# A hybrid recurrent decoder step on one core: norm rows made in columns, and the last weight group split into prompt and sample columns

## The chip, the cores and the metric

The kernel runs on one NeuronCore of a Trainium2 chip. Its engines are named as in the profile: PE is TensorE (matmul), PEld its weight load, DVE is VectorE, ACT is ScalarE, POOL is GpSimd, SP is SyncE, which mostly issues DMAs. The metric is the device time of one execution in microseconds (us); lower is better.

## The reference

One inference step of a two-layer decoder trunk over two groups of tokens: 256 prompt tokens with zero initial state, and 8 sequences of 8 sample tokens with given states. So there are 320 token columns, and the model width is 2048. All is float32.

- Layer 0: `h = rmsnorm(x)`, one input projection of `h` to 7,200 columns; eight gated-delta heads and four GLA heads run over it; `x += W_out[...]`.
- Layer 1: `h = rmsnorm(x)`, a projection to 4,096 columns (branch and gate), a convolution over 4 tokens, an RG-LRU scan, a gate; `x += W_out[...]`.
- `y = rmsnorm(x) * final_norm` for both groups, beside the new states.

The part that the change touches is the norm, three times:

```
def _rmsnorm(x, g):
    xf = x.astype(jnp.float32)
    y = xf * lax.rsqrt(jnp.mean(xf * xf, axis=-1, keepdims=True) + EPS)
    return (y * g.astype(jnp.float32)).astype(x.dtype)
```

## The kernel before

**Tiling.** Activations are kept transposed: the 2048 features lie on 128 partitions times 16 tiles, the 320 tokens along the free dimension (columns 0 to 255 prompt, 256 to 319 sample). The residual is `ob[m][:, f, :]`, four tiles of four blocks. All dense weights come as 30 groups of 512 output features; a group has 8 chunks of 2 feature tiles, 512 KB each. `run_group` (line 250) walks a group: for each chunk, for each of four 128-feature blocks `f`, for both tiles `a`, it issues one *product* (line 259).

**A product is three matmuls (line 265).** Weights and activations are split into a high and a low part in the fp32r type: `wh`, `wl` and `xh`, `xl`. The product is `wh*xh + wh*xl + wl*xh`, with the 128x128 weights stationary and 320 activation columns moving. The four blocks of a group accumulate in four PSUM banks (`acc`, four buffers). Weights are split on the fly by `split_chunk` (line 235): ScalarE writes `wh` (L240), VectorE writes `wl` (L241), two chunks ahead, into six buffers of each; SP loads chunks four ahead into three buffers (L210).

**Order of the work.** Everything beside the dense products is written as generators in four lists, `hi`, `lo`, `lo2` and `tails`. After each product there is a *slot* (line 130), which advances the first generator of each list by one step. `wait(name)` yields as many slots as the table `WAITS` says; with it the distance between the steps of a piece of side work is set. The instructions so written are then put in order for each engine by a planner, by priority and by its own costs; splits and evacuations have raised priority (`HP`, `HE`). Each engine executes its list in order, so that an instruction that waits holds back all behind it. `behind(i)` keeps a side matmul from being planned ahead of the latest product.

**The norms.** The gain is folded into the activations and the row of `1/rms` is applied to the products afterwards. The first two norms go through `row_rstd` (line 335): one matmul of all-ones weights over the summed squares gives each token's sum on all partitions, in 320 columns; ScalarE scales it and takes the root (L340, L341); VectorE takes the reciprocal (L343), and GpSimd refines it by a Newton step (L344 to L347). The first makes `rb0`, beside groups 0 and 1, and its first readers are L355 and L356 in `evac_padded` (line 352), which the convolution taps (L464) and ScalarE's L101 follow. The second makes `rb1`, needed at the end of the first group of layer 1. The row `rb0` is read also by all later evacuations of layer 0.

**The final norm and the tail.** `evac_fin` (line 1639) adds the residual (L1642) for the last four groups; for the last it squares each block (L1645). `last` (line 1680) sums the squares per token with the squares as weights (`sums`, L1677), so that tokens lie on partitions in three columns, raises them to -1/2 (L1686) and spreads them back over columns by `spread_rows` (line 326, L331). Lines 1919 to 1928 then multiply the sixteen blocks by that row, VectorE most of them (L1927), GpSimd two (L1923), each followed by its store (eight on SP's queue, one on ScalarE's).

Beside the last four groups run the GLA sample states (`sample_states(16, 24)`, line 992), with matmuls of their own at L1132; those of the delta states (L1118) ran beside earlier groups in the same way.

Of the kernel before, what the change touches and what calls it, by code (L numbers as in the profile page):

```python
# [7 lines left out]
F32 = mybir.dt.float32  # L8
# [63 lines left out]
def hybrid_step(ctx, tc, x_cols, w_dense, w_small, w_lr, w_gate, par_a, par_b, par_c, gains, head_rows,  # L72
# [21 lines left out]
    def bank(name):  # L94
        return psum.tile([P, 512], F32, name=name, tag="bg", bufs=4)

    def bank4(name):
        return psum.tile([P, 4, P], F32, name=name, tag="bg", bufs=4)

    def scaled(out, in_, scale):  # L100
        return act.activation(out, in_, AF.Identity, scale=scale)  # L101
# [64 lines left out]
    eps = const.tile([P, 1], F32, name="eps")  # L166
# [68 lines left out]
    def split_chunk(i, a):  # L235
        if i >= len(chunks):
            return
        h = wpool.tile([P, 512], F32R, name="wh", tag="wh", bufs=6)
        l = wpool.tile([P, 512], F32R, name="wl", tag="wl", bufs=6)
        act.activation(h, wst[i][:, a, :], AF.Copy)  # L240
        env["last_split"] = dve.tensor_sub(l, wst[i][:, a, :], h.bitcast(F32))  # L241
# [84 lines left out]
    def spread_rows(ps, r):  # L326


        for c in range(3):
            n, a = (P, 0) if c < 2 else (64, 64)  # L330
            mm = pe.matmul(ps[:, c * P:c * P + n], r[:, c:c + 1].to_broadcast([P, P]), ident[:, a:a + n],  # L331
                           start=True, stop=True)
            behind(mm)

    def row_rstd(v, t, sq, out, nm):

        ps = bank(nm + "ps")
        behind(pe.matmul(ps[:, :NT], ones, sq, start=True, stop=True))
# [4 lines left out]
        dve.reciprocal(out, out)  # L343
        pool.tensor_mul(t, out, out)  # L344
        pool.tensor_mul(t, t, v)
        pool.tensor_scalar(t, t, -0.5, 1.5, op0=OP.mult, op1=OP.add)
        pool.tensor_mul(out, out, t)  # L347
# [67 lines left out]
    def slab():  # L415
        return env["keep"].tile([P, 4, XA], F32, name="slab", tag="slab", bufs=1)
# [1028 lines left out]
    def evac_res(m):  # L1445
        st = {}

        def before():
            def load():
                st["x0"] = env["ws2"].tile([P, 4, NT], F32, name="x0r", tag="x0r", bufs=1)  # L1450
                yield from wait("resid.1")
                for f in (0, 2):
                    behind(sp.dma_start(st["x0"][:, f:f + 2], x_cols[m, :, f:f + 2]))
                    yield from wait("fill.2")
            tails.append(load())

        def evac(f, acc):
            if f == 0:
                drain(tails)
            dve.tensor_add(ob[m][:, f, :], acc[:, :NT], st["x0"][:, f, :])  # L1460

        def sumsq():
            ws = env["ws2"]
            sq = ws.tile([P, 4, NT], F32, name="sq", tag="sq", bufs=1)
            act.activation(sq, ob[m], AF.Square)
            yield from wait("evac_res_sumsq.1")
            if m == 0:
                env["sqa"] = ws.tile([P, NT], F32, name="sqa", tag="sqa", bufs=1)
                dve.tensor_reduce(env["sqa"], sq.rearrange("p f t -> p t f"), axis=mybir.AxisListType.X, op=OP.add)
            else:  # L1470
                s1 = ws.tile([P, NT], F32, name="sq1", tag="sq1", bufs=1)
                dve.tensor_reduce(s1, sq.rearrange("p f t -> p t f"), axis=mybir.AxisListType.X, op=OP.add)
                dve.tensor_add(env["sqa"], env["sqa"], s1)
            yield from wait("evac_res_sumsq.2")
            env["done"].add(("x", m))
            if m == 3:
                yield from row_rstd(sq[:, 0], sq[:, 1], env["sqa"], rb1, "r1")
# [160 lines left out]

    def evac_fin(m):
        def evac(f, acc):  # L1640
            x = ob[m][:, f, :]
            dve.tensor_add(x, acc[:, :NT], x)  # L1642
            if m == 3:
                sq = fin["sq"]
                i = act.activation(sq[:, f, :], x, AF.Square)  # L1645
                if f < 2:
                    dve.tensor_add(fin["sqa"], fin["sqa"], sq[:, f, :])
                else:
                    with tc.issue_after(i.ins):
                        gain(f - 2)  # L1650
                    if f == 3:
                        fin["last"] = i

        def gain(f):
            i = scaled(ob[3][:, f, :], ob[3][:, f, :], pb[:, 12 + f, 42:43])
            return i

        def work():
            sq = fin["sq"]
# [14 lines left out]
        def sums(sq, i):  # L1674
            for c in range(3):
                a = min(c * P, NT - P)
                pe.matmul(fin["ps"][:, c, :], sq[:, a:a + P], ones,  # L1677
                          start=(i == 0 and c == 0), stop=(i == 2), skip_group_check=True)

        def last():  # L1680
            fin["ps"] = bank4("fsp")
            for i, sq in enumerate((fin["sqa"], fin["sq"][:, 2, :], fin["sq"][:, 3, :])):
                sums(sq, i)
            fr = fin["fr"]
            dve.tensor_scalar(fr, fin["ps"][:, 0:3, 0], 1.0 / D, EPS, op0=OP.mult, op1=OP.add)
            pool.tensor_tensor(fr, fr, mhalf[:, :3], OP.pow)  # L1686
            fin["row"] = [bank("frow") for _ in range(2)]
            for ps in fin["row"]:
                spread_rows(ps, fr)
            with tc.issue_after(fin["last"].ins):  # L1690
                for f in (2, 3):
                    gain(f)
            yield

        def after():
            if m < 3:
                tails.append(work())
            else:
                drain(tails)
                hi.append(last())  # L1700
        return None, evac, after

    for m in range(4):
# [67 lines left out]
    def start_work():  # L1771
# [14 lines left out]
        yield from row_rstd(sums[:, 1], sums[:, 2], sums[:, 0], rb0, "r0")  # L1786
# [116 lines left out]
    shut(lru_p, mid_p)  # L1903
    fin_p, fw = opened("fin", "right")
    env["ws2"] = fw
    fin["fr"] = fw.tile([P, 3], F32, name="fr")
    fin["sqa"] = fw.tile([P, NT], F32, name="fsqa")
    fin["sq"] = slab().rearrange("p f w -> p (f w)")[:, :4 * NT].rearrange("p (f t) -> p f t", f=4)
    env["upd"] = fw
    lo.append(sample_states(16, 24))  # L1910
# [1 line left out]
    for k in range(2):  # L1912
        one(k)
    run_group(next(gi), rest)
    for _ in range(3):
        run_group(next(gi))
    drain(hi)
    drain(tails)
    drain(lo)
    row = fin["row"][0][:, :NT]  # L1920
    rows = fw.tile([P, NT], F32, name="frows")
    act.activation(rows, fin["row"][1][:, :NT], AF.Copy)
    pool.tensor_mul(ob[3][:, 0:2], ob[3][:, 0:2], rows[:, None, :].to_broadcast([P, 2, NT]))  # L1923
    act.dma_start(y_cols[3, :, 0:2], ob[3][:, 0:2])
    for m, f, n in ((0, 0, 1), (0, 1, 1), (0, 2, 2), (1, 0, 2), (1, 2, 2), (2, 0, 2), (2, 2, 2), (3, 2, 2)):
        t = ob[m][:, f:f + n]
        dve.tensor_mul(t, t, row[:, None, :].to_broadcast([P, n, NT]))  # L1927
        sp.dma_start(y_cols[m, :, f:f + n], t)
# [62 lines left out]
```

## Time and profile before

| | |
|---|---|
| median of 3 runs | 988.08 us (986.78 to 988.36) |
| the profiled execution's own time | 988.05 us |
| its span | 985.9 us |
| mean granted TensorE clock | 0.994 |
| DMA over the span | 171.62 MB, mean 174 GB/s |

How to read it: a row of a timeline has the start in us from the start of the span, the time taken, the engine, the line of the kernel, the operation, what it writes and reads, the shapes, how many instructions are merged in the row, and in brackets how long the engine stood idle before and what released it. A row of a group has, behind the bar, the busy time in us, the mean of one instruction in ns, and the idle time before. A row of a wait has the engine, tile and line that waited, who ended the wait, the total in us, the number of times and the longest. A plain float32 matmul shows as two instructions (two passes). Matmuls are pipelined, and the time shown for one is longer than the distance from one start to the next.

### The profile page before, as it was taken

The numbers are of one execution on the slowest core, as the hardware profiler recorded it, in microseconds if no ns is written. First come the engines' busy times: TensorE is split into PE (matmuls) and PEld (weight loads), VectorE is DVE, ScalarE is ACT, GpSimd is POOL, SyncE is SP. The second block draws the span as 40 slices with busy tenths as digits, with TensorE's granted clock in tenths as the row PEclk, the third lists the DMA queues.
The fourth block names the chain that finished last, engine by engine and source line by source line (L and its number), as shares of the span: only waits on it lengthen the run. The fifth ranks groups of instructions, "written<-read, shape, count | busy, mean of one in ns | idle before, by whom it ended". The sixth has DMA issues, their size and how long they took to land.

```text
span 985.9 us, 18789 instructions
## 1 busy us (share of the span) xinstructions
PE 968.4 (98%) x6917; PEld 951.9 (97%) x6917; DVE 708.9 (72%) x1485; ACT 534.7 (54%) x1084; POOL 216.6 (22%) x365
## 2 busy tenths in 40 slices
PE   9999999999999999999999999999999999999995
PEld 9988999999999999999979999999999999999995
DVE  7897887675555557689658789777969668876753
ACT  8556874456433454676523335447685885343441
POOL 6420027602182021120104234200010000042200
PEclk9999999999999999999999999999999999999998
DMA  8544345443546367444477886654545445588742
GB/s 307 171 133 136 111 140 170 140 126 122 142 150 166 98 212 234 125 120 140 164 249 254 254 264 222 228 161 140 159 123 191 129 128 161 170 245 267 255 151 106
DMA packets 65331, 171.62 MB, mean 174 GB/s; under 512 B 16884, under 2 KB 22536, under 8 KB 64728
## 3 DMA queue, kind: packets, MB, share of 16 engines
q1 hardware_dynamic: 60256, 160.35, 52.3%
q0 software_dynamic: 2720, 8.66, 2.5%
q10 hardware_dynamic: 2264, 1.42, 0.5%
q8 instruction: 54, 0.88, 0.4%
q14 instruction: 37, 0.30, 0.1%
HBM read 155.73 MB, written 14.68 MB: 173 GB/s over the span
## 4 chain that ended last, share of the span: by engine, by line
PE 86%; DVE 4%; ACT 3%; issue 3%; DMA 2%; POOL 1%; SPq 0%; DVEq 0%; ACTq 0%; POOLq 0%
PE acc L265 75%; DVE wl L241 1%; ACT wh L240 1%; DMA wst<-in_w_dense_dram 1%; DMA XT<-xt_scratch 1%; DVE ob L1927 0%; POOL xsums L1782 0%; PE gpo L1368 0%; PE lg L1556 0%; PE lg L1557 0%; PE lg L1555 0%; DVE yc L464 0%; PE gsn L1132 0%; PE po L844 0%; PE sn L1118 0%
## 5 line engine op out<-in xcount | busy, mean ns | idle before, releaser
L265 PE MATMUL acc<-xh,wh 128*128 128x320 f32 x1920 | 602.0, 314 | 0.2 <-ACT wh L231 0.2
L265 PE MATMUL acc<-xh,wl 128*128 128x320 f32 x1920 | 595.2, 311 | 3.2 <-DVE wl L241 3.2
L265 PE MATMUL acc<-xl,wh 128*128 128x320 f32 x1920 | 596.3, 311 | 0.0
L240 ACT ACTIVATE wh<-wst 128x512 fp32r<-128x512 f32 x479 | 279.6, 623 | 311.4 <-PE acc L265 253.5
L241 DVE TENSOR_TENSOR wl<-wst,wh 128x512 fp32r<-128x512 f32 x479 | 334.5, 728 | 143.6 <-ACT wh L240 140.9
L265 PEld LDWEIGHTS acc<-xh,wl 128*128 128x128 f32 x1920 | 361.7, 189 | 4.2 <-DVE wl L241 3.7
L265 PEld LDWEIGHTS acc<-xh,wh 128*128 128x128 f32 x1920 | 362.1, 189 | 2.8 <-issue 1.3
L265 PEld LDWEIGHTS acc<-xl,wh 128*128 128x128 f32 x1920 | 362.5, 189 | 1.4
L464 DVE SCALAR_TENSOR_TENSOR yc<-slab,pa,yc 128x344 f32<-128x344 f32 x72 | 42.2, 610 | 1.9 <-ACT yc L101 1.5
L703 POOL TENSOR_TENSOR xi<-xi,tmp 128x60 f32<-128x60 f32 (+24 forms) x62 | 26.3, 425 | 4.9
L1584 POOL MEMSET aa<- 128x32 f32 x4 | 0.7, 162 | 117.7 <-ACT rr L1571 66.7
L701 POOL TENSOR_TENSOR tmp<-ab,xi 128x60 f32<-128x60 f32 (+24 forms) x62 | 24.7, 399 | 4.8
L1122 DVE SCALAR_TENSOR_TENSOR ust<-ust,es,sn 128x128 f32<-128x128 f32 x64 | 18.2, 339 | 3.8 <-PE sn L1118 2.2
L1013 POOL TENSOR_TENSOR uvkh<-uvk,uvkh 32x256 fp32r<-32x256 f32 (+1 forms) x8 | 8.4, 1049 | 57.2 <-DMA uvk<-vk_scratch 48.1
L1018 POOL TENSOR_TENSOR uvm<-uvh,rm 96x512 fp32r<-96x512 f32 x16 | 19.5, 1241 | 2.8 <-PE sn L1118 2.5
L758 POOL TENSOR_TENSOR so<-so,mhalf 128x4 f32<-128x4 f32 x4 | 4.4, 1104 | 71.3 <-DVE so L757 71.3
L101 ACT ACTIVATE yc<-slab,pa 128x344 f32<-128x344 f32 x24 | 13.5, 578 | 11.3 <-DVE slab L356 10.0
L1136 DVE SCALAR_TENSOR_TENSOR ugt<-ugt,ebs,gsn 128x256 f32<-128x256 f32 x32 | 14.1, 476 | 6.0 <-PE gsn L1132 6.0
L468 ACT ACTIVATE qkv<-yc 128x256 f32<-128x256 f32 x24 | 10.0, 417 | 15.2 <-DVE yc L464 15.1
L1515 DVE SCALAR_TENSOR_TENSOR yc<-slab,pb,yc 128x344 f32<-128x344 f32 x32 | 17.6, 575 | 0.7 <-ACT yc L1513 0.6
L1125 POOL DMA_DIRECT2D out_s_delta_dram<-ust x8 | 6.0, 751 | 50.5 <-DVE ust L1122 50.5
L355 DVE TENSOR_TENSOR slab<-acc,rb 128x256 f32<-128x256 f32 x36 | 15.0, 418 | 2.7 <-PE acc L265 2.7
(464 smaller groups left out, 1011.1 us busy)
## 6 DMA issues: line engine op xcount, KB each, us to landing
wst<-in_w_dense_dram SPq DMA_DIRECT2D x237, 512.0 KB, 3.6
st<-in_state_delta_dram SPq DMA_DIRECT2D x8, 512.0 KB, 7.1
st<-in_state_gla_dram SPq DMA_DIRECT2D x4, 1024.0 KB, 7.0
ust<-in_state_delta_dram SPq DMA_DIRECT2D x8, 512.0 KB
out_s_delta_dram<-ust POOLq DMA_DIRECT2D x8, 512.0 KB, 4.9
ugt<-in_state_gla_dram SPq DMA_DIRECT2D x8, 512.0 KB, 7.5
out_s_gla_dram<-ugt POOLq DMA_DIRECT2D x8, 512.0 KB, 4.8
x0r<-in_x_cols_dram SPq DMA_DIRECT2D x8, 320.0 KB, 5.1
```

The costliest lines, as they stand in the source:

```text
L101: return act.activation(out, in_, AF.Identity, scale=scale)
L240: act.activation(h, wst[i][:, a, :], AF.Copy)
L241: env["last_split"] = dve.tensor_sub(l, wst[i][:, a, :], h.bitcast(F32))
L265: mm = pe.matmul(o, (h, h, l)[j][:, fs], (xh, xl, xh)[j][k], start=(k == 0 and j == 0), stop=(k == KT - 1 and j == 2))
L355: dve.tensor_mul(xp[:, 3:259], xp[:, 3:259] if acc is None else acc[:, :256], rb[:, :256])
L464: dve.scalar_tensor_tensor(y[:, :n], xp[:, j:j + n], pa[:, ft, j:j + 1], y[:, :n], op0=OP.mult, op1=OP.add)
L701: behind(pool.tensor_mul(tv, ab[:, j, j + 1:, None].to_broadcast([P, m, w]), xi[:, j:j + 1, :w].to_broadcast([P, m, w])))
L703: behind(pool.tensor_add(xi[:, j + 1:, :w], xi[:, j + 1:, :w], tv))
L1018: pool.tensor_mul(m, src.bitcast(F32)[:, None, :].to_broadcast([R, 4, P]), rm4[:R, :, None].to_broadcast([R, 4, P]))
L1122: dve.scalar_tensor_tensor(s_, s_, es[:, col:col + 1], ps[:, b, :], op0=OP.mult, op1=OP.add)
L1136: dve.scalar_tensor_tensor(s_, s_, ebs[:, h, 4 * hb + b + i:4 * hb + b + i + 1], ps[:, i * 256:(i + 1) * 256], op0=OP.mult, op1=OP.add)
L1515: dve.scalar_tensor_tensor(y[:, :n], xp[:, j:j + n], pb[:, ft, 2 + j:3 + j], y[:, :n], op0=OP.mult, op1=OP.add)
```

## The change

**Norm rows in columns.** `row_rstd` now works as the final norm does: `token_sums` uses the summed squares as weights and gives the sums with tokens on partitions, in three columns; `root` does the small VectorE step and GpSimd's power; `spread_rows` brings them back to a row, and ScalarE copies it out of PSUM. The table of waits has 1, 7 and 1 slots for it in place of 0 and 5.

**The last group.** `run_last` takes the place of `run_group` for the thirtieth group. Products have only the 256 prompt columns, in two PSUM banks. The 64 sample columns are made the other way round: `fxs` holds, for each of the 16 feature tiles, 64 columns of `xh` and 64 of `xl` side by side (written by `beside` during the two groups before), and is used as weights, while `wh` and `wl` move with 512 columns each. That gives samples on 64 partitions for the high part and on 64 for the low one; a `fold` matmul with two stacked identities adds the two and transposes back, on top of the residual. The first eight feature tiles' sample matmuls are issued within the group, the last eight (`KEPT`) behind it, between the steps of the prompt's norm; the last chunk's split weights get buffers of their own. The prompt's norm, products and stores come first, then the samples' own norm, products and stores. Final results are written to the `hs` tiles, and `y_cols` in memory has the prompt part of each feature block first and the sample part behind.

```diff
-    "row_rstd.1": 0, "row_rstd.2": 5, ...
+    "row_rstd.1": 1, "row_rstd.2": 7, "row_rstd.3": 1, ...
...
+        k = 2 * (i - len(chunks) + 8) + a
+        if k >= KT - KEPT + 6:
+            h, l = [fin["w"].tile([P, 512], F32R, name=f"{n}{k}") for n in ("wh", "wl")]
...
+    def run_last(g):
+        two = [psum.tile([P, 2, TP], F32, name="acc", tag="acc", bufs=4) for _ in range(2)]
+        accs = [two[f % 2][:, f // 2] for f in range(4)]
+        sacc = psum.tile([P, 512], F32, name="sacc", tag="acc", bufs=4)
+        early = KT - KEPT
+
+        def samples(k):
+            h, l = whl[len(chunks) - 8 + k // 2, k % 2]
+            for j, w in enumerate((h, l)):
+                behind(pe.matmul(sacc, fin["xs"][:, k], w, start=(k == 0 and j == 0), stop=(k == KT - 1 and j == 1)))
+
+        for kc in range(8):
...
+                    for j in range(3):
+                        mm = pe.matmul(accs[f], (h, h, l)[j][:, fs], (xh, xl, xh)[j][k][:, :TP],
+                                       start=(k == 0 and j == 0 and f < 2), stop=(k == KT - 1 and j == 2),
+                                       skip_group_check=True)
...
+            for k in (2 * kc, 2 * kc + 1):
+                if k < early:
+                    samples(k)
+        g["after"]()
+        drain(hi)
+        drain(tails)
+        drain(lo)
...
+        run(4)
+        ps = bank4("fsp")
+        sq = fin["sq"]
+        for i, q in enumerate((fin["sqa"][:, :TP], sq[:, 2, :TP], sq[:, 3, :TP])):
+            token_sums(ps, q, i == 0, i == 2)
+        root(rr[:, 0:2], ps[:, 0:2, 0])
+
+        fold = psum.tile([P, 4, TS], F32, name="fold", tag="acc", bufs=4)
+        for f in range(4):
+            behind(pe.matmul(fold[:, f], ident, ob[3][:, f, TP:], start=(f == 0), stop=False, skip_group_check=True))
+        pss = bank("fss")
+        behind(pe.matmul(pss[:TS, :TS], fin["sqa"][:, TP:], ones[:, :TS], start=True, stop=False))
+        run(1)
+        with tc.issue_after(fin["last"].ins):
+            for f in (2, 3):
+                gain(f)
+        rows = [bank("frow") for _ in range(2)]
+        for r in rows:
+            spread_rows(r, rr[:, 0:2])
+        run(KEPT - 5)
...
+        act.activation(row2, rows[1][:, :TP], AF.Copy)
+        act.activation(sev[:, 0:2], sacc[:, 0:256], AF.Copy)
+        act.activation(sev[:, 2:4], sacc[:, 256:512], AF.Copy)
+        for f in range(4):
+            pe.matmul(fold[:, f], sev[:, f], fin["fold"], start=False, stop=(f == 3), skip_group_check=True)
...
+        for f in (0, 1):
+            prompt(3, f, 1, pool, row2)
+        for m, f in ((0, 0), (0, 2), (1, 0), (1, 2), (2, 0)):
+            prompt(m, f)
+            store(m, f, 2, sp)
+        store(3, 0, 2, sp)
+        i = act.activation(ssq, fold, AF.Square)
+        for f in range(4):
+            pe.matmul(pss[:TS, :TS], ssq[:, f], ones[:, :TS], start=False, stop=(f == 3))
+        with tc.issue_after(i.ins):
+            for f in range(4):
+                scaled(ob[3][:, f, TP:], fold[:, f], pb[:, 12 + f, 42:43])
+        root(rr[:TS, 2:3], pss[:TS, 0:1])
+        for m, f in ((2, 2), (3, 2)):
+            prompt(m, f)
+            store(m, f, 2, sp)
+        row = bank("frs")
+        pe.matmul(row[:, :TS], rr[:TS, 2:3].to_broadcast([TS, P]), ident[:TS, :TS], start=True, stop=True)
+        act.activation(row3, row[:, :TS], AF.Copy)
+        sample(0, dve, row, act)
+        sample(2, pool, row3, act)
+        sample(1, dve, row, sp)
+        sample(3, dve, row, act)
...
-    def row_rstd(v, t, sq, out, nm):
-        ps = bank(nm + "ps")
-        behind(pe.matmul(ps[:, :NT], ones, sq, start=True, stop=True))
+    def token_sums(ps, sq, start, stop):
+        n = sq.shape[1]
+        for c in range((n + P - 1) // P):
+            a = min(c * P, n - P)
+            behind(pe.matmul(ps[:, c, :], sq[:, a:a + P], ones, start=start and c == 0, stop=stop,
+                             skip_group_check=True))
+    def root(r, ps):
+        dve.tensor_scalar(r, ps, 1.0 / D, EPS, op0=OP.mult, op1=OP.add)
+        pool.tensor_tensor(r, r, mhalf[:r.shape[0], :r.shape[1]], OP.pow)
+    def row_rstd(sq, out, nm):
+        ps = bank4(nm + "ps")
+        token_sums(ps, sq, True, True)
         yield from wait("row_rstd.1")
-        act.activation(v, ps[:, :NT], AF.Identity, scale=1.0 / D, bias=eps[:, 0:1])
-        act.activation(out, v, AF.Sqrt)
+        root(rr, ps[:, 0:3, 0])
         yield from wait("row_rstd.2")
-        dve.reciprocal(out, out)
-        pool.tensor_mul(t, out, out)
-        pool.tensor_mul(t, t, v)
-        pool.tensor_scalar(t, t, -0.5, 1.5, op0=OP.mult, op1=OP.add)
-        pool.tensor_mul(out, out, t)
+        row = bank(nm + "row")
+        spread_rows(row, rr)
+        yield from wait("row_rstd.3")
+        act.activation(out, row[:, :NT], AF.Copy)
...
+    def beside():
+        for k in range(KT):
+            act.activation(fin["xs"][:, k, :TS], xh[k][:, TP:].bitcast(F32), AF.Copy)
+            pool.tensor_copy(fin["xs"][:, k, TS:], xl[k][:, TP:].bitcast(F32))
+            yield from wait("fill.2")
+    hi.append(beside())
+    for _ in range(2):
         run_group(next(gi))
     drain(hi)
...
+    run_last(next(gi))
```

More of the change, by code (lines that the diff above doesn't have):

```diff
@@ L34 @@
 HE = 50
+KEPT = 8
 NA0 = 2
@@ L237, in split_chunk @@
             return
-        h = wpool.tile([P, 512], F32R, name="wh", tag="wh", bufs=6)
-        l = wpool.tile([P, 512], F32R, name="wl", tag="wl", bufs=6)
+        k = 2 * (i - len(chunks) + 8) + a
+        if k >= KT - KEPT + 6:
+            h, l = [fin["w"].tile([P, 512], F32R, name=f"{n}{k}") for n in ("wh", "wl")]
+        else:
+            h = wpool.tile([P, 512], F32R, name="wh", tag="wh", bufs=6)
+            l = wpool.tile([P, 512], F32R, name="wl", tag="wl", bufs=6)
         act.activation(h, wst[i][:, a, :], AF.Copy)
@@ L244, in hybrid_step, with run, prompt, store @@
     pos = [0]
+    def run_last(g):
[8 more added lines that the diff above has]
+        for kc in range(8):
+            i = pos[0]
+            pos[0] += 1
+            for f in range(4):
+                for a in range(2):
+                    k = 2 * kc + a
+                    h, l = whl[i, a]
+                    fs = slice(f * P, (f + 1) * P)
+                    for j in range(3):
+                        mm = pe.matmul(accs[f], (h, h, l)[j][:, fs], (xh, xl, xh)[j][k][:, :TP],
+                                       start=(k == 0 and j == 0 and f < 2), stop=(k == KT - 1 and j == 2),
+                                       skip_group_check=True)
+                    marks.append(mm.ins)
+                    if a == 0:
+                        slot()
+                if f == 1:
+                    load_chunk(i + 4)
+                if kc == 7:
+                    with tc.high_priority(offset=HE):
+                        g["evac"](f, accs[f])
+                if f % 2 == 0:
+                    with tc.high_priority(offset=HP):
+                        for c in ahead(i):
+                            split_chunk(c, f // 2)
+                slot()
+            for k in (2 * kc, 2 * kc + 1):
[5 more added lines that the diff above has]
+        drain(lo)
+        gain, out = fin["gain"], [t.rearrange("p f t -> p (f t)") for t in env["hs"]]
+        outp = [t[:, :4 * TP].rearrange("p (f t) -> p f t", f=4) for t in out]
+        outs = [t[:, 4 * TP:].rearrange("p (f t) -> p f t", f=4) for t in out]
+        late = iter(range(early, KT))
+        def run(n):
+            for _ in range(n):
+                samples(next(late))
+        run(4)
[17 more added lines that the diff above has]
+        run(KEPT - 5)
+        sev, ssq, row2, row3 = [fin["w"].tile(d, F32, name=n) for n, d in (
+            ("sev", [P, 4, P]), ("ssq", [P, 4, TS]), ("frow2", [P, TP]), ("frow3", [P, TS]))]
+        act.activation(row2, rows[1][:, :TP], AF.Copy)
[3 more added lines that the diff above has]
+            pe.matmul(fold[:, f], sev[:, f], fin["fold"], start=False, stop=(f == 3), skip_group_check=True)
+        def prompt(m, f, n=2, eng=dve, row=rows[0]):
+            o = outp[m][:, f:f + n]
+            eng.tensor_mul(o, ob[m][:, f:f + n, :TP], row[:, None, :TP].to_broadcast([P, n, TP]))
+        def store(m, f, n, q):
+            q.dma_start(y_cols[m, :, f * TP:(f + n) * TP], outp[m][:, f:f + n])
+        def sample(m, eng, row, q):
+            eng.tensor_mul(outs[m], ob[m][:, :, TP:], row[:, None, :TS].to_broadcast([P, 4, TS]))
+            q.dma_start(y_cols[m, :, 4 * TP:], outs[m])
+        for f in (0, 1):
[8 more added lines that the diff above has]
+        with tc.issue_after(i.ins):
+            for f in range(4):
+                scaled(ob[3][:, f, TP:], fold[:, f], pb[:, 12 + f, 42:43])
[10 more added lines that the diff above has]
+        sample(3, dve, row, act)
@@ L326, in spread_rows @@
     def spread_rows(ps, r):
-        for c in range(3):
+        for c in range(r.shape[1]):
             n, a = (P, 0) if c < 2 else (64, 64)
@@ L1476, in sumsq @@
             if m == 3:
-                yield from row_rstd(sq[:, 0], sq[:, 1], env["sqa"], rb1, "r1")
+                yield from row_rstd(env["sqa"], rb1, "r1")
                 env["done"].add("r1")
@@ L1640, in evac @@
         def evac(f, acc):
-            x = ob[m][:, f, :]
-            dve.tensor_add(x, acc[:, :NT], x)
+            n = acc.shape[1] if m == 3 else NT
+            x = ob[m][:, f, :n]
+            dve.tensor_add(x, acc[:, :n], x)
             if m == 3:
-                sq = fin["sq"]
-                i = act.activation(sq[:, f, :], x, AF.Square)
+                sq = fin["sq"][:, f, :n]
+                i = act.activation(sq, x, AF.Square)
                 if f < 2:
-                    dve.tensor_add(fin["sqa"], fin["sqa"], sq[:, f, :])
+                    dve.tensor_add(fin["sqa"][:, :n], fin["sqa"][:, :n], sq)
                 else:
@@ L1654, in gain @@
         def gain(f):
-            i = scaled(ob[3][:, f, :], ob[3][:, f, :], pb[:, 12 + f, 42:43])
-            return i
+            x = ob[3][:, f, :TP]
+            return scaled(x, x, pb[:, 12 + f, 42:43])
         def work():
@@ L1672, in work @@
                 yield from wait("evac_fin_work.4")
[L1674 to L1693, printed above, removed]
         def after():
@@ L1699, in after @@
                 drain(tails)
-                hi.append(last())
+                fin["gain"] = gain
         return None, evac, after
@@ L1785, in start_work @@
         yield from wait("start_work.2")
-        yield from row_rstd(sums[:, 1], sums[:, 2], sums[:, 0], rb0, "r0")
+        yield from row_rstd(sums[:, 0], rb0, "r0")
         behind(dve.tensor_mul(smw, smw, gcol[:, :, None].to_broadcast([P, KT, 32])))
@@ L1905, in hybrid_step @@
     env["ws2"] = fw
-    fin["fr"] = fw.tile([P, 3], F32, name="fr")
     fin["sqa"] = fw.tile([P, NT], F32, name="fsqa")
+    fin["w"] = fw
+    fin["xs"] = fw.tile([P, KT, P], F32R, name="fxs")
+    fin["fold"] = fw.tile([P, TS], F32, name="ffold")
+    dve.tensor_add(fin["fold"], ident[:, :TS], ident[:, TS:])
     fin["sq"] = slab().rearrange("p f w -> p (f w)")[:, :4 * NT].rearrange("p (f t) -> p f t", f=4)
@@ L1914, in hybrid_step @@
     run_group(next(gi), rest)
-    for _ in range(3):
+    def beside():
[5 more added lines that the diff above has]
+    for _ in range(2):
         run_group(next(gi))
     drain(hi)
[L1918 to L1928, printed above, removed]
+    run_last(next(gi))
     shut(fin_p, keep_p)
-_OUTS = [("y_cols", (4, 128, 4, NT)), ("p_delta", (8, 128, 128)), ("p_gla", (4, 128, 256)),
+_OUTS = [("y_cols", (4, 128, 4 * NT)), ("p_delta", (8, 128, 128)), ("p_gla", (4, 128, 256)),
          ("s_delta", (8, 128, 8, 128)), ("s_gla", (4, 128, 8, 256)), ("dconv", (128, 24, 27)),
```

6 lines of the change are left out of this document (3 added, 3 removed), and 2 rows, old and new, of the table WAITS.

## The prediction

> **What bounds the kernel now.** I read the page first, then who waited for whom on TensorE, then the stretches where it lost time, and the last 16 us in order of time.
>
> ```profile
> span 985.9 us, 18789 instructions
> ...
> PE 968.4 (98%) x6917; PEld 951.9 (97%) x6917; DVE 708.9 (72%) x1485; ACT 534.7 (54%) x1084; POOL 216.6 (22%) x365
> ...
> PE 86%; DVE 4%; ACT 3%; issue 3%; DMA 2%; POOL 1%; SPq 0%; DVEq 0%; ACTq 0%; POOLq 0%
> ```
>
> TensorE is busy 98% of the span and is 86% of the chain that ended last. Work on another engine pays only where TensorE stands still, and each matmul added to its stream costs its full time. It stands still in few places:
>
> ```profile
> PE acc L265 <- DVE wl L241: 3.2, 2, 2.0
> ...
> PE cum L538 <- DVE gt L531: 0.6, 1, 0.6
> ```
>
> The first is the one that the change can reach. In order of time, TensorE and then VectorE, GpSimd and ScalarE around it:
>
> ```profile
> 58.44 0.31 PE L265 MATMUL acc<-xl,wh 128*128 128x320 f32 x1
> 60.78 0.42 PE L265 MATMUL acc<-xh,wl 128*128 128x320 f32 x1 [2.03 <-DVE wl L241]
> ...
> 49.13 2.14 DVE L343 RECIPROCAL rb<-rb 128x320 f32<-128x320 f32 x1
> ...
> 55.23 0.42 DVE L355 TENSOR_TENSOR slab<-slab,rb 128x256 f32<-128x256 f32 x1 [2.29 <-POOL rb L347]
> ...
> 60.04 0.69 DVE L241 TENSOR_TENSOR wl<-wst,wh 128x512 fp32r<-128x512 f32 x1
> ...
> 51.36 1.04 POOL L344 TENSOR_TENSOR xsums<-rb 128x320 f32<-128x320 f32 x1 [8.95 <-DVE rb L343]
> ...
> 54.31 0.88 POOL L347 TENSOR_TENSOR rb<-rb,xsums 128x320 f32<-128x320 f32 x1
> ...
> 55.83 1.05 ACT L101 ACTIVATE yc<-slab,pa 128x344 f32<-128x344 f32 x2 [4.77 <-DVE slab L356]
> ```
>
> The norm row rb0 is ready only at 55.2. Until then VectorE stands 2.29 us at L355 and ScalarE 4.77 us behind it, each with weight splits queued behind the waiting instruction. The split that ends at 60.7 is what TensorE waits for from 58.4. The stall is dearer than its idle time, as the two stretches of low clock show (columns: time, then busy time and instructions of PE, PEld, DVE, ACT, POOL, the granted clock, DMA):
>
> ```profile
> 60.78:65.36 4.58, 4.58 (x20) 4.58 (x21) 4.58 (x11) 3.74 (x9) 0.00 (x0) 0.63 0.58 160
> 95.43:99.55 4.12, 4.12 (x20) 4.12 (x20) 3.38 (x7) 0.90 (x2) 0.00 (x0) 0.59 0.13 34
> ```
>
> Twenty matmuls took 4.58 and 4.12 us at granted clocks 0.63 and 0.59. At the pace of the last group (below: three in 0.44 us, 0.1465 each) they take 2.93, so the low clock cost 1.65 and 1.19 us.
>
> The tail, after the last product:
>
> ```profile
> 970.70 0.31 PE L265 MATMUL acc<-xh,wl 128*128 128x320 f32 x1
> ...
> 971.14 0.31 PE L265 MATMUL acc<-xh,wl 128*128 128x320 f32 x1
> ...
> 972.32 1.50 PE L1677 MATMUL fsp<-ones,slab 128*128 128x128 f32 x12
> ...
> 973.86 0.16 DVE L1685 TENSOR_SCALAR fr<-fsp 128x3 f32<-128x3 f32 x1 [1.89 <-PE fsp L1677]
> 974.11 0.90 POOL L1686 TENSOR_TENSOR fr<-fr,mhalf 128x3 f32<-128x3 f32 x1 [24.95 <-DVE fr L1685]
> ...
> 975.98 5.27 DVE L1927 TENSOR_TENSOR ob<-ob,frow 128x320 f32<-128x320 f32 x8 [1.96 <-PE frow L331]
> 976.49 5.68 SPq L1928 DMA_DIRECT2D out_y_cols_dram<-ob  x8
> ...
> 977.00:978.00 1.00, 0.00 (x0) 0.00 (x0) 1.00 (x2) 0.08 (x1) 0.84 (x1) 1.00 0.61 219
> 979.00:980.00 1.00, 0.00 (x0) 0.00 (x0) 1.00 (x3) 0.00 (x0) 0.00 (x0) 1.00 1.03 394
> 984.00:985.00 1.00, 0.00 (x0) 0.00 (x0) 0.00 (x0) 0.00 (x0) 0.00 (x0) 0.50 0.34 136
> ```
>
> From 979 the stores run at 394 GB/s with all DMA engines busy. They end near 984.35 (0.34 of the last stretch), and the span 1.55 us later. So the old tail is bound by store bandwidth, once the first store is out.
>
> **Part 1: norm rows in columns (twice).** Removed per norm: one matmul over 320 columns, two ScalarE passes with a table load, a reciprocal of 2.14 us, four GpSimd passes (51.36 to 55.19). Added: three token sums, a small VectorE step, a GpSimd power over three columns (0.90, the row at 974.11), three spreading matmuls and a ScalarE copy. On TensorE:
>
> ```profile
> 42.80 0.70 PE L338 MATMUL r0ps<-xsums,ones 128*128 128x320 f32 x2
> ...
> 43.48 0.31 PE L265 MATMUL acc<-xl,wh 128*128 128x320 f32 x1
> ...
> L1677 PE MATMUL fsp<-ones,slab 128*128 128x128 f32 x12 | 1.5, 275 | 0.0
> ```
>
> The old matmul runs as two passes; 43.48 − 42.80 less one product (0.147) is 0.53 us. A pass over 128 columns costs (1.50 − 0.275)/11 = 0.111, from the twelve at 972.32, the last of which takes its 0.275 to its end. Six matmuls are 12 passes, 1.33 us. So each norm **adds 0.8 us** of TensorE, 1.6 for both. Cheaper bound: 64 columns in the last spread, 0.1 us less; dearer: a wait for the power, a rival below.
>
> The gain at the first norm: the power can be done about 1.3 us after the sums (0.16 + 0.90 and gaps), near 46, if VectorE takes the small step when ready. The spread is placed eight slots after the sums, a slot being three matmuls, 0.44 us: 43.5 + 3.5 = 47.0, and the copy follows near 48.5. That is 6.7 us before 55.2, and VectorE loses the 2.14 us reciprocal as well; the split ending at 60.7 needs to come only 2.3 us earlier. I take the whole stall: 60.78 − 58.44 − 0.147 = 2.19 idle plus 1.65 low clock, **3.84 us saved**. The bounds are 0 and 3.84 plus the second hold-up (0.6 + 1.19).
>
> At the second norm nothing waits, so only the 0.8 us remains:
>
> ```profile
> 638.10 1.19 POOL L347 TENSOR_TENSOR rb<-rb,sq 128x320 f32<-128x320 f32 x1
> ...
> 641.73 0.42 DVE L355 TENSOR_TENSOR slab<-acc,rb 128x256 f32<-128x256 f32 x1
> ```
>
> The row was there at 639.3, its first reader came at 641.73.
>
> **Part 2: the last group.** Prompt products shrink from 320 to 256 columns; sample columns return as 32 matmuls of 512 columns, 16 inside the group and 16 behind it. The nearest rows of both sizes:
>
> ```profile
> 932.51 0.40 PE L1132 MATMUL gsn<-uvkh,uvm 96*128 96x256 f32 x2
> 932.75 0.31 PE L265 MATMUL acc<-xh,wh 128*128 128x320 f32 x1
> ...
> 528.94 0.40 PE L1118 MATMUL sn<-uvm,ukh 96*128 96x512 f32 x1
> 529.18 0.31 PE L265 MATMUL acc<-xh,wh 128*128 128x320 f32 x1
> ```
>
> Two of 256 take 0.24, one of 512 takes 0.24. The group: 192 × (0.1465 − 0.12) = 5.09 less, 16 × 0.24 = 3.84 more. The last prompt product starts at 971.14 − 1.25 = 969.9 (all times here without part 1). [...]
>
> Other prices:
>
> ```profile
> L1172 POOL TENSOR_TENSOR gso<-gso,mhalf 128x1 f32<-128x1 f32 x10 | 5.4, 543 | 0.8
> L468 ACT ACTIVATE qkv<-yc 128x256 f32<-128x256 f32 x24 | 10.0, 417 | 15.2 <-DVE yc L464 15.1
> L355 DVE TENSOR_TENSOR slab<-acc,rb 128x256 f32<-128x256 f32 x36 | 15.0, 418 | 2.7 <-PE acc L265 2.7
> 940.00:960.00 20.00, 20.00 (x140) 20.00 (x139) 12.21 (x23) 8.97 (x15) 0.53 (x1) 1.00 0.47 158
> 976.86 4.39 DVE ob L1927 x6
> ```
>
> *Prompt chain.* Four late pairs' worth (8 × 0.24) to 971.9 cover the last residual add and square (0.42 each after 970.2). Twelve sum passes to 973.3; VectorE and a power over two columns (between 0.54 and 0.90, 0.7) to 974.45. Meanwhile TensorE does ten small passes (1.1) and two late matmuls (0.48), to 974.85; four spread passes, and VectorE starts at 975.5 instead of 975.98. A store then follows each 512-element product (0.73 per 640 elements, so 0.60 each, 437 GB/s, above the 394 that drain).
>
> *Sample chain.* Four more spread passes, six late matmuls: 977.3. Two ScalarE copies of 256 columns, 978.1. Eight folding passes, 979.2. A square, 979.65. Eight sum passes, 980.7. VectorE and the one-column power (0.54), 981.55. Spread, 981.95. Three VectorE products (0.42, then 0.33 each) beside a ScalarE copy and a GpSimd product, 983.1. ScalarE then issues three stores one after the other (0.34 each), the last from about 983.6; data follows 0.9 after an issue (976.49 to about 977.4), 131 KB take 0.35, and the end comes 1.55 later: **986.4, against 985.9: +0.5.** The stores grow from 9 to 12, the prompt's eight are drained by about 983. Bounds: with the stores alone deciding, 0.6 less than before (the start 0.5 earlier); with the 18 small passes at half speed, 2.0 more than my value.
>
> The sixteen ScalarE and sixteen GpSimd copies that lay the sample weights side by side run in the two groups before, where in 20 us ScalarE is busy 8.97 and GpSimd 0.53; uncovered they would cost 16 × 0.24 on ScalarE at most.
>
> **Sum,** on the profiled execution's 988.05 (span 985.9; the median shown is 988.08): 988.05 − 3.84 + 1.6 + 0.5 = **986.3**.
>
> **Rivals.**
> - *Second hold-up goes too:* the wait of 0.6 at L538 and its 1.19 of low clock, as ScalarE and VectorE come out of the first norm without a backlog. Against: that chain starts from a matmul and moves with it. 984.5.
> - *TensorE waits at the new spread (slower):* VectorE holds other work, and it took the reciprocal at 49.13. If it takes the small step only then, the power ends at 50.3, TensorE stands at L331's spread from 47.0, 3.3 us, with products behind it, and 1.65 of low clock: 986.3 + 4.9 = 991.2. It begins when the power ends after 47.0 and makes the kernel slower from some 2 us of wait, low clock included.
> - *The change doesn't reach the stall:* VectorE's own load (busy 4.58 of 4.58 above) keeps the split late. 990.1.
> [...]
> - *A slow sample chain,* small passes at half speed: 988.3.
>
> **How the numbers follow.** Forecast 0.45, with its own range 985.1 to 987.7; second hold-up 0.20; wait at the spread 0.13; stall not reached 0.07; low clock stays 0.07; slow sample chain 0.08. What can be told from no change is 0.2%, 2.0 us, so faster is below 986.1. The forecast lies just above that: somewhat under half of its 0.45, the whole 0.20 and 0.02 of the others make faster 0.44; slower, above 990.0, is 0.10 of the wait and 0.04 of the stall, 0.14; the rest, 0.42, is the same. The range reaches from the second hold-up's going (984.5 less 1.2) to most of the wait: 983.3 to 990.6.
>
> **What would show it.** TensorE without a wait on wl between 50 and 65 and no low clock there; rb0 written near 48 to 49; twelve passes around each norm without a wait in front of the spread; the last group's products 0.12 apart; VectorE's first final product 0.5 us earlier, counted from the old last product; the last store from ScalarE, after the prompt's. It is wrong if a low clock or wait stands anywhere in 45 to 65, or if stores still saturate the DMA to the end.

## The result: 0.18% slower, and the profile after

| | before | after |
|---|---|---|
| median of 20 runs each | 987.87 us (986.50 to 989.36, and one of 1470.29) | 989.11 us (987.05 to 991.61) |
| ratio after / before, 95% interval | | 1.0018 [1.0011, 1.0025] |
| the profiled execution's own time | 988.05 us | 987.99 us |

Forecast was 986.3. The medians differ by 1.24 us; the ratio, which leaves out the one execution of 1470.29, puts the difference at 0.18%, 1.8 us. That lies within the 0.2% that the prediction took for what can be told from no change, but over 20 runs each the interval leaves no change out, and the sign is the other one. The two profiled executions differ by 0.06 us only, so the profile must be read by stretches. The page of after, and who waited for whom on TensorE (engine, tile, line, releaser: us in total, times, longest):

```profile
span 985.8 us, 18967 instructions
...
PE 972.1 (99%) x6987; PEld 954.2 (97%) x6987; DVE 704.3 (71%) x1488; ACT 536.2 (54%) x1104; POOL 219.5 (22%) x378
...
PE 91%; ACT 3%; DVE 3%; issue 1%; DMA 1%; POOL 0%; SPq 0%; DVEq 0%; ACTq 0%; POOLq 0%
```

```profile
PE r0row L453 <- POOL rr L467: 2.3, 1, 2.3
...
PE acc L387 <- DVE wl L246: 1.1, 1, 1.1
```

TensorE still carries the span, 99% busy and 91% of the chain that ended last. Of the waits for `wl`, 3.2 us in two before, the one of 2.0 at 58.4 is gone. A wait of 2.3 has come at the new spread, L453, for the power. The first norm in order of time:

```profile
42.41 0.83 PE L462 MATMUL r0ps<-ones,xsums 128*128 128x128 f32 x6
43.00 0.39 PE L387 MATMUL acc<-xh,wh 128*128 128x320 f32 x1
...
46.45 0.31 PE L387 MATMUL acc<-xh,wl 128*128 128x320 f32 x1
...
46.82 0.17 DVE L680 TENSOR_SCALAR nclam<-clam 128x16 f32<-128x16 f32 x1
...
47.54 0.15 DVE L466 TENSOR_SCALAR rr<-r0ps 128x3 f32<-128x3 f32 x1
...
47.78 1.26 POOL L467 TENSOR_TENSOR rr<-rr,mhalf 128x3 f32<-128x3 f32 x1 [5.75 <-DVE rr L466]
...
49.09 0.88 PE L453 MATMUL r0row<-ident,rr 128*128 128x128 f32 x6 [2.34 <-POOL rr L467]
...
50.01 0.44 ACT L479 ACTIVATE rb<-r0row 128x320 f32<-128x320 f32 x1 [2.73 <-PE r0row L453]
```

The sums are done by 43.24 (42.41 + 0.83), but VectorE takes the small step at 47.54. Until 47.0 it works mostly through a chain of tiny steps for the decay constants (`clam`, `nclam`; about 0.2 us each), which stand ahead of it in its list, and then through a split. The power ends at 49.04. TensorE reaches its spread near 46.7 and stands, with all products of its list behind the waiting matmul. The granted clock of the stretches around it (us, then busy time of PE, PEld, DVE, ACT, POOL, clock, DMA share, GB/s):

```profile
46.73:50.14 3.41, 1.07 (x9) 1.05 (x9) 2.73 (x7) 0.68 (x2) 1.26 (x1) 1.00 0.30 76
50.14:53.55 3.41, 3.41 (x15) 3.41 (x14) 3.05 (x9) 2.06 (x4) 0.00 (x0) 0.50 0.54 156
53.55:56.97 3.42, 3.42 (x25) 3.42 (x24) 1.76 (x4) 1.93 (x3) 0.00 (x0) 1.00 0.30 116
...
981.98:985.39 3.41, 0.00 (x0) 0.00 (x0) 0.23 (x1) 0.00 (x0) 0.00 (x0) 0.50 0.48 162
```

For 3.41 us after the stop TensorE has half the clock: 15 matmuls where 25 follow in as long a stretch behind it. In that window matmuls start 0.267 us apart (50.43, 50.69, 50.96) in place of 0.1465, so the window costs 3.41 × (1 − 0.1465/0.267) = 1.54 us. (The last row, in the tail, is used further below.) So one stall has been exchanged for another of the same kind. What was gained at 58.4 was spent at 46.7, and the added passes and the tail remain.

The later rows, for the other terms, which are read in the part on the prediction:

```profile
627.87 0.83 PE L462 MATMUL r1ps<-ones,sqa 128*128 128x128 f32 x6
679.38 0.31 PE L1687 MATMUL lg<-xch,waxh 128*128 128x320 f32 x1
...
873.80 0.40 PE L1264 MATMUL gsn<-uvkh,uvm 96*128 96x256 f32 x2
...
969.16 0.28 PE L273 MATMUL acc<-xl,wh 128*128 128x256 f32 x1
969.28 0.28 PE L273 MATMUL acc<-xh,wl 128*128 128x256 f32 x1
...
975.00 3.68 DVE L335 TENSOR_TENSOR hs<-ob,frow 128x512 f32<-128x512 f32 x6 [2.04 <-PE frow L453]
...
981.93 1.34 ACTq L342 DMA_DIRECT2D out_y_cols_dram<-hs  x3
```

### The profile page after: what moved, and what is told of

The parts are those of the page before. It is cut to its first block, busy times and chain, and to the rows that moved or that the text cites. A ratio compares the mean times of both kernels' runs of the same rounds, so it can differ in the third digit from the quotient of the medians.

```text
span 985.8 us, 18967 instructions
## 1 busy us (share of the span) xinstructions
PE 972.1 (99%) x6987; PEld 954.2 (97%) x6987; DVE 704.3 (71%) x1488; ACT 536.2 (54%) x1104; POOL 219.5 (22%) x378
## 4 chain that ended last, share of the span: by engine, by line
PE 91%; ACT 3%; DVE 3%; issue 1%; DMA 1%; POOL 0%; SPq 0%; DVEq 0%; ACTq 0%; POOLq 0%
PE acc L387 77%; PE acc L273 2%; DVE wl L246 1%; DMA wst<-in_w_dense_dram 1%; PE sacc L262 1%; ACT wh L245 1%; PE gpo L1500 0%; PE lg L1688 0%; PE lg L1689 0%; PE lg L1687 0%; PE gsn L1264 0%; PE po L976 0%; PE pq L1064 0%; PE sn L1250 0%; PE y L967 0%
## 5 line engine op out<-in xcount | busy, mean ns | idle before, releaser
L387 PE MATMUL acc<-xh,wh 128*128 128x320 f32 x1856 | 580.5, 313 | 0.0
L387 PE MATMUL acc<-xh,wl 128*128 128x320 f32 x1856 | 574.0, 310 | 1.2 <-DVE wl L246 1.1
L387 PE MATMUL acc<-xl,wh 128*128 128x320 f32 x1856 | 574.8, 310 | 0.0
L387 PEld LDWEIGHTS acc<-xh,wh 128*128 128x128 f32 x1856 | 349.4, 188 | 2.4 <-issue 1.3
L387 PEld LDWEIGHTS acc<-xh,wl 128*128 128x128 f32 x1856 | 348.7, 188 | 2.2 <-DVE wl L246 1.7
L387 PEld LDWEIGHTS acc<-xl,wh 128*128 128x128 f32 x1856 | 349.4, 188 | 1.2
L273 PE MATMUL acc<-xh,wh 128*128 128x256 f32 x64 | 18.2, 284 | 0.0
L273 PE MATMUL acc<-xh,wl 128*128 128x256 f32 x64 | 18.1, 282 | 0.0
L273 PE MATMUL acc<-xl,wh 128*128 128x256 f32 x64 | 18.1, 282 | 0.0
```

The costliest lines, as they stand in the source:

```text
L273: mm = pe.matmul(accs[f], (h, h, l)[j][:, fs], (xh, xl, xh)[j][k][:, :TP], start=(k == 0 and j == 0 and f < 2), stop=(k == KT - 1 and j == 2),
L387: mm = pe.matmul(o, (h, h, l)[j][:, fs], (xh, xl, xh)[j][k], start=(k == 0 and j == 0), stop=(k == KT - 1 and j == 2))
```

## The experiments

**Theory A:** the loss is the wait at the first norm's spread, because VectorE takes the small step late. **Theory B:** the new tail costs it. **Theory C,** for the first experiment: a row that comes later holds the splits as in before, and the old stall at 58 returns. The first four kernels ran on one chip with 35 runs of before between them (median 987.27).

**1. The spread placed later.** After, with thirteen slots in place of seven between small step and spread.

```diff
-    "row_rstd.1": 1, "row_rstd.2": 7, "row_rstd.3": 1,
+    "row_rstd.1": 1, "row_rstd.2": 13, "row_rstd.3": 1,
```

> The changed kernel with the spread of the first two norms placed six slots later (13 in place of 7), 2.6 us. Theory A (TensorE waits at the first norm's spread for the power, 2.5 us idle, and a stretch of low clock of some 1.2 to 1.6 us follows): no wait at the spread, rb0 written about as late as now (near 50), no new wait on wl; 3 to 4 us less than the changed kernel, about 985.5, and 2 us less than the kernel before. Theory B (the loss is in the tail, the samples' own norm): nothing moves, 989. Theory C (a late row holds the splits, as before): the old stall at 58 returns, 988 to 989.

Measured: 987.38 us, ratio to before 1.0003 [0.9992, 1.0013].

```profile
43.12 0.83 PE L462 MATMUL r0ps<-ones,xsums 128*128 128x128 f32 x6
...
48.50 1.26 POOL L467 TENSOR_TENSOR rr<-rr,mhalf 128x3 f32<-128x3 f32 x1 [5.76 <-DVE rr L466]
...
49.95 0.78 PE L453 MATMUL r0row<-ident,rr 128*128 128x128 f32 x6
...
51.23 0.43 DVE L487 TENSOR_TENSOR slab<-slab,rb 128x256 f32<-128x256 f32 x1 [0.40 <-ACT rb L479]
...
374.19 1.96 PE L1064 MATMUL pq<-st,qm 128*32 128x128 f32 x64
```

The wait is gone, and by the ratios 1.5 us of the time with it (1.1 by the medians). No wait stands near 58, so theory C is out. The gain is less than was expected. From the sums to the first `pq` (the first query product of the head states, a point that all kernels pass) it takes 331.07 us, 1.4 more than in the next experiment. Small waits further down are a part of it:

```profile
119.05 0.42 PE L387 MATMUL acc<-xh,wl 128*128 128x320 f32 x1 [0.42 <-DVE wl L246]
...
129.18 0.49 PE L779 MATMUL kk<-qkv 128*128 128x128 f32 x2 [0.50 <-ACT dtm L765]
```

Over the whole stretch TensorE is idle for 1.96 us here and for 1.33 in experiment 2, which has some small waits of its own; so waits make up 0.6 of the 1.4, and the rest wasn't located. The row's first reader starts 8.1 us behind the start of the sums (51.23 − 43.12), as late as in after; that this lateness causes these waits was not followed up. Placing the spread later hides a late small step; it doesn't make the step earlier.

**2. The small step ahead of the chain.** After, with the decay constants' steps put behind the small step on VectorE; TensorE's order is as in after, matmul for matmul in the two traces.

```diff
-        dve.tensor_scalar(r, ps, 1.0 / D, EPS, op0=OP.mult, op1=OP.add)
+        env["step"] = dve.tensor_scalar(r, ps, 1.0 / D, EPS, op0=OP.mult, op1=OP.add)
...
-        softplus_small(ws, clam, nclam, [P, 16], "spl")
-        dve.tensor_scalar(clam, clam, 8.0, None, op0=OP.mult)
-        dve.tensor_scalar(nclam, clam, -1.0, None, op0=OP.mult)
+        with tc.issue_after(env["step"].ins):
+            softplus_small(ws, clam, nclam, [P, 16], "spl")
+            dve.tensor_scalar(clam, clam, 8.0, None, op0=OP.mult)
+            dve.tensor_scalar(nclam, clam, -1.0, None, op0=OP.mult)
```

> The changed kernel, with VectorE's small step of the first norm ordered ahead of the chain of tiny lambda steps that it now stands behind; the matmuls keep their order. Theory A: the step moves from 47.5 to about 44.5, the power ends near 46, TensorE does not wait at the spread, rb0 is there near 48; 3 to 4 us less than the changed kernel, about 985.5. Theory B: nothing moves, 989. If GpSimd's power and not the step's place is what is late, about 1 us less than the changed kernel.

Measured: 986.07 us, ratio 0.9988 [0.9978, 0.9998].

```profile
43.61 0.94 PE L462 MATMUL r0ps<-ones,xsums 128*128 128x128 f32 x6 [0.34 <-POOL xsums L1896]
...
44.59 0.16 DVE L466 TENSOR_SCALAR rr<-r0ps 128x3 f32<-128x3 f32 x1
...
44.83 0.88 POOL L467 TENSOR_TENSOR rr<-rr,mhalf 128x3 f32<-128x3 f32 x1 [1.27 <-DVE spls L430]
...
47.91 0.78 PE L453 MATMUL r0row<-ident,rr 128*128 128x128 f32 x6
...
373.30 1.95 PE L1065 MATMUL pq<-st,qm 128*32 128x128 f32 x64
```

The step comes 0.98 us behind the start of the sums (in after 5.13), the power ends 2.2 us before the spread, and TensorE doesn't wait there. By the ratios this is 3.0 us below after (2.4 by the medians), at the lower end of what theory A said. From the sums to the first `pq` it takes 329.69 us; experiment 1 took 331.07. In after the same stretch is 333.13 and in before 333.56:

```profile
375.54 1.95 PE L1064 MATMUL pq<-st,qm 128*32 128x128 f32 x64
```

```profile
376.36 1.84 PE L932 MATMUL pq<-st,qm 128*32 128x128 f32 x60
```

After is 3.44 us longer than experiment 2. The wait and the half-clock window make 3.88 (2.34 and 1.54). Less 0.34 for a wait in experiment 2 that after doesn't have (below), that is 3.54, so nearly all of the difference is located. Before holds in this stretch the old wait of 2.03 and two half-clock windows (shown further below), 5.11 in all; after holds 3.88 and 0.8 of added passes, 4.68. The 0.43 between these sums is the measured difference (333.56 − 333.13). So the profiled execution of before has one half-clock window more here than that of after, which helps to explain why the two profiles come out alike while the medians don't.

```profile
272.50 0.39 PE L387 MATMUL acc<-xh,wh 128*128 128x320 f32 x1 [0.34 <-DVE smpkb L1289]
```

**3. The tail alone.** The norms of before (L338 to L347 of before) with the new last group.

```diff
-        yield from row_rstd(sums[:, 0], rb0, "r0")
+        yield from row_rstd_old(sums[:, 1], sums[:, 2], sums[:, 0], rb0, "r0")
...
-                yield from row_rstd(env["sqa"], rb1, "r1")
+                yield from row_rstd_old(sq[:, 0], sq[:, 1], env["sqa"], rb1, "r1")
```

> The new last group and tail, with both norm rows made as before. Theory A: the tail costs 0.3 to 0.5 us, so 988.3 against 987.9 for the kernel before. Theory B: the whole loss of 1.2 to 1.8 us is here, 989 to 990.

Measured: 987.51 us, ratio 1.0003 [0.9993, 1.0012]. The tail costs 0.3 us by its middle value, which is not to be told from nothing; theory B asked for 1.2 to 1.8 us, and only the end of the interval reaches 1.2. The old stall is there again, in this execution without low clock (its row in time, and then three stretches; the last is in the tail):

```profile
61.86 0.41 PE L388 MATMUL acc<-xh,wl 128*128 128x320 f32 x1 [2.13 <-DVE wl L247]
```

```profile
57.23:60.64 3.41, 2.50 (x18) 2.24 (x16) 3.41 (x9) 3.06 (x5) 0.00 (x0) 1.00 0.02 8
60.64:64.05 3.41, 2.19 (x15) 2.19 (x16) 3.41 (x10) 3.06 (x9) 0.00 (x0) 1.00 0.32 73
...
982.24:985.65 3.41, 0.00 (x0) 0.00 (x0) 0.45 (x2) 0.00 (x0) 0.14 (x1) 0.50 0.56 189
```

**4. The norms alone.** Before, with the new `row_rstd` and its three helpers, and the old last group.

```diff
-    "row_rstd.1": 0, "row_rstd.2": 5,
+    "row_rstd.1": 1, "row_rstd.2": 7, "row_rstd.3": 1,
...
-        yield from row_rstd(sums[:, 1], sums[:, 2], sums[:, 0], rb0, "r0")
+        yield from row_rstd(sums[:, 0], rb0, "r0")
```

> The new norm rows alone, with the last group and tail as before. Theory A: the stall of 3.8 us at 58 is gone, 1.6 us of matmuls are added, and a wait of 2.5 with some 1.5 of low clock stands at the spread, so 0.3 to 1.5 us more than the kernel before, 988.2 to 989.4. Theory B: the gain of the norms as forecast, 985.7.

Measured: 988.60 us, ratio 1.0014 [1.0004, 1.0024]. With experiment 3 this adds to 1.0017; after has 1.0018. By the middle values the loss is in the norms, and the wait is there:

```profile
PE r0row L331 <- POOL rr L345: 2.5, 1, 2.5
```

```profile
47.32:50.73 3.41, 1.37 (x11) 1.38 (x12) 2.45 (x5) 0.55 (x3) 1.26 (x1) 1.00 0.36 94
50.73:54.14 3.41, 3.41 (x15) 3.41 (x14) 3.40 (x9) 1.69 (x3) 0.00 (x0) 0.50 0.53 157
```

**5 to 8. The other terms of the sum.** Each keeps the small step first. One has the second norm as before, one has the last group as before, one has both as before; experiment 2 ran again beside them (on another chip than the first four, with 34 runs of before, median 987.11). The second norm is taken back in after with this edit:

```diff
-                yield from row_rstd(env["sqa"], rb1, "r1")
+                yield from row_rstd_old(sq[:, 0], sq[:, 1], env["sqa"], rb1, "r1")
```

The two kernels with the last group as before were made from before: one has both norms of experiment 4, the other only the first of them, and both have the step of experiment 2.

> Small step first at the first norm, new last group, but the second norm made as before. Theory (each new norm costs 0.8 us of added TensorE passes where nothing waits): r1ps to lg falls back by 0.8 us, and the time is 0.8 us below the kernel that differs only in the second norm. Rival (the second norm is free or gains by unloading GpSimd and ScalarE): the same time or more.

> Small step first, both norms new, the last group and the tail as before. Theory (the new tail is 0.3 to 0.5 us longer than the old one): 0.3 to 0.5 us below the kernel that differs only in the tail, near 985.7. Rival (the tail is no longer): no difference or a loss.

> Only the first norm is new, with its small step first; second norm, last group and tail as before. Both terms of the sum that cost time are gone, so theory: 1.1 to 1.3 us below the kernel with all three parts and the small step first, 2 to 2.5 us below before, about 985. If it is not the lowest of these four, the two terms don't add.

> All parts of the change and the small step first, on the chip of the three kernels it is compared with. Expected as in its first measurement: ratio to before 0.9988, some 1.2 us below before.

| first norm, step first, and | median | ratio to before |
|---|---|---|
| second norm and last group new (experiment 2 again) | 986.16 | 0.9992 [0.9982, 1.0002] |
| second norm as before | 985.19 | 0.9978 [0.9970, 0.9987] |
| last group as before | 985.81 | 0.9987 [0.9978, 0.9995] |
| both as before | 985.15 | 0.9975 [0.9966, 0.9984] |

Taking the second norm back gains 1.0 us with the new last group and 0.7 with the old one, against 0.8 expected. Taking the last group back gains 0.35 and 0.04, against 0.3 to 0.5. The intervals of these four overlap, so each single difference is only consistent with its term. The last kernel has the lowest median, though only by 0.04 us, which doesn't tell it from the one with the new last group. With a ratio of 0.9975 it beats before, by 2.5 us (2.0 by the medians), and, by the ratios, after. The repeat of experiment 2 reaches just above 1; its two measurements, 0.9988 and 0.9992, agree. The second norm's stretch with the old form in place:

```profile
626.60 0.78 PE L485 MATMUL r1ps<-sqa,ones 128*128 128x320 f32 x2 [0.58 <-DVE sqa L1621]
...
677.37 0.31 PE L1703 MATMUL lg<-xch,waxh 128*128 128x320 f32 x1
```

From the second sums to the first `lg` it takes 50.77 us with the old form here; in after it took 679.38 − 627.87 = 51.51, in before 679.85 and 629.12, 50.73:

```profile
629.12 0.74 PE L338 MATMUL r1ps<-sqa,ones 128*128 128x320 f32 x2
...
679.85 0.31 PE L1555 MATMUL lg<-xch,waxh 128*128 128x320 f32 x1
```

## Why the prediction was wrong, point by point

**The gain at the first norm: the step that failed.** The prediction says: "the power can be done about 1.3 us after the sums (0.16 + 0.90 and gaps), near 46, if VectorE takes the small step when ready." VectorE doesn't. In after the sums were done at 43.24, but the step stood behind the chain of tiny steps and a split in VectorE's list; it came at 47.54 and the power ended at 49.04. The chain could have been read in the trace of before, where it lasts until 47.4, two splits and one more operation follow, and the reciprocal comes at 49.13:

```profile
47.21 0.17 DVE L548 TENSOR_SCALAR nclam<-clam 128x16 f32<-128x16 f32 x1
47.32 1.29 DVE L241 TENSOR_TENSOR wl<-wst,wh 128x512 fp32r<-128x512 f32 x2
```

The condition "if VectorE takes the small step when ready" was written down and not looked up. It was safe to ignore in before, where ScalarE made root and scaling and VectorE was needed only at 49.13. The change moved VectorE into the middle of the norm and put a TensorE instruction behind it. Experiment 2 meets the condition: the step comes at 44.59, the power ends at 45.71, and the median is 1.2 us below before, where the forecast had 1.7.

**The rival that came true** is the wait at the new spread, held at 0.13. Its mechanism is right, and its size roughly: 2.34 us of wait for 3.3, from the step at 47.54 and not 49.13, and a power of 1.26 us for the 0.90 taken. It gave 991.2; the median is 989.11. The rivals that the stall isn't reached and that the sample chain is slow didn't come.

**The stall on `wl`: right in itself.** With rb0 written from 50.01 in after, the stall at 58 is gone. The 3.84 us of the sum (2.19 idle, 1.65 low clock) were mis-sized as a fixed price: the idle time is there in both traces that have the stall (2.03 us in before, 2.13 in experiment 3), the low clock behind it only in before.

**The low clock: wrong in kind.** It was taken as a fixed price behind the stall. These are the stretches of before, cut where its clock changes:

```profile
58.44:61.85 3.41, 1.38 (x10) 1.11 (x9) 3.41 (x10) 2.73 (x7) 0.00 (x0) 1.00 0.03 10
61.85:65.26 3.41, 3.41 (x15) 3.41 (x14) 3.41 (x8) 2.75 (x8) 0.00 (x0) 0.50 0.73 199
92.57:95.98 3.41, 2.82 (x20) 2.09 (x19) 2.80 (x11) 2.18 (x3) 0.00 (x0) 1.00 0.62 166
95.98:99.39 3.41, 3.41 (x15) 3.41 (x15) 2.84 (x6) 0.63 (x1) 0.00 (x0) 0.50 0.05 4
```

In front of the tail each low clock of before and after lasted 3.41 us: from 61.85 to 65.26, from 95.98 to 99.39, and in after from 50.14 to 53.55. Their starts lie whole numbers of such windows apart, as on a grid: with 3.413 us for one, 95.98 − 61.85 = 34.13 is ten of them, and in after 981.98 − 50.14 = 931.84, from there to the low clock of the tail, is 273. Counted back from 982.24 (270 windows), where the clock of experiment 3 falls in its tail, a boundary there would lie at 60.64, in the middle of the stall; this place is an estimate from those distances. The two windows beside it keep 2.50 and 2.19 us of TensorE work, and no low clock follows. In before, after and experiment 4 one window takes nearly the whole stop, 1.38, 1.07 and 1.37 us of work are left, and the next window has half the clock. So in these four traces a stop of some 2.3 us cost that alone or, with the 1.54 of the next window, about 3.9, as the grid fell. The 20 executions of after point the same way: the 12 with a mean granted clock of 0.996 or less took 990.0 us in the mean, the other 8 took 988.2. Of experiment 2's 12, with the same tail, 11 lie above 0.996. Low clock in the tail is in these means too, so this is a hint and no count of windows.

TensorE still worked in the window in front of the low clock (1.07 of 3.41 us in after, 1.38 at the stall of before). The prediction gave 0.07 to a low clock that stays whatever becomes of the stall. That is not borne out: the one behind the stall (61.85 to 65.26 in before) went with it, and one came with the new wait (50.14 to 53.55 in after).

**The added passes: right.** From the second sums to `lg` the change is +0.78 us, for +0.8. The six token sums held the next product for 43.00 − 42.41 = 0.59 us.

**The last group: right.** The products are 0.12 apart (969.16, 969.28). From the last GLA matmul group of the states, at 873.80 (before 874.27), to the last prompt product it takes 95.48 us, for 96.87 before: 1.39 less, for 1.25. From the last prompt product VectorE's first final product comes 5.72 us later, for 975.5 − 969.9 = 5.6, and the span ends 16.52 us later, for 986.4 − 969.9 = 16.5. The sample chain does set the end, as said: DMA falls to 102 GB/s from 982 to 983, while the samples' stores are being issued.

```profile
982.00:983.00 1.00, 0.00 (x0) 0.00 (x0) 0.21 (x1) 0.00 (x0) 0.00 (x0) 0.50 0.29 102
983.00:984.00 1.00, 0.00 (x0) 0.00 (x0) 0.00 (x0) 0.00 (x0) 0.00 (x0) 0.50 1.02 340
```

**The range** held the median, thanks to the rival of the wait; the median lies in what the prediction counts as the same, up to 990.0. The 0.13 for the wait was too small, since its condition could be looked up.

What stays open: the second hold-up, near 92 to 96. Its wait of 0.6 us on `gt` stayed in after. In before it was followed by low clock although its window was 2.82 us busy (above), so low clock didn't come only behind windows that are mostly idle. No low clock follows it in after, nor in the first execution of experiment 2 (clock 1.00 from 90 to 100 in both); in the repeat, with the same kernel, one does, and in the kernel with both as before (0.50 from 93.79 to 97.20). The rows of the repeat:

```profile
88.60:92.01 3.41, 2.81 (x20) 1.99 (x19) 2.81 (x11) 1.92 (x3) 0.00 (x0) 1.00 0.59 167
92.01:95.42 3.41, 3.41 (x14) 3.41 (x14) 3.14 (x7) 0.89 (x2) 0.00 (x0) 0.50 0.03 12
```

TensorE's order is the same in both executions. The repeat is 1.45 us ahead of the first at the start of this half-clock window (as at the first norm's sums, 42.16 and 43.61) and 0.02 ahead at its end (0.01 at the `kk` group behind it, 130.71 and 130.72); the difference, 1.43, is the price of the window in the same kernel. So the loss there can come and go between executions of one kernel. What decides it was not found, and no kernel was made to test it.

## What to carry to other kernels

When an edit moves a small step to another engine and makes TensorE wait for it, read what stands in that engine's list around the place: here the input was ready at 43.24, and VectorE took the step at 47.54, behind the chain and a split. Put such a step ahead of work that isn't due (experiment 2: taken at 44.59), or put the waiting matmul far enough behind it (experiment 1: no wait at the spread). And price a stop of TensorE as a span, from its idle time alone (2.13 us in experiment 3) to that plus a half-clock window (2.34 and 1.54 in after), not as one value from one profile.

## What the runs showed of the hardware

In front of the tail, each low clock of before and after lasted 3.41 us at a granted clock of 0.50, and the starts lay whole multiples of 3.413 us apart (34.13 and 931.84). One such window cost 1.54 us in after and 1.43 between the two executions of experiment 2. In the four traces read here, a stop of TensorE (2.03 us in before, 2.34 in after, 2.5 in experiment 4) brought one where it fell into one window; in experiment 3 (2.13), where the grid counted back cuts it in two, none came. GpSimd's power over three columns took 1.26 us in after and in experiment 1, beside 512-wide work of VectorE, and 0.88 in experiment 2, beside tiny steps; that VectorE's work is the reason wasn't tested.
